# Triangular inverses from single blocks, swapped attention products and aligned tiles in a hybrid decoder block

## The chip, the cores and the metric

The kernel runs on one core of a Trainium2 chip. The metric is the device time of one launch in microseconds (us). A core has TensorE (PE in the profile, its weight loads apart as PEld), VectorE (DVE), ScalarE (ACT), GpSimd (POOL) and SyncE (SP, which here issues the weight DMAs). Each engine works through its own list of instructions in order; semaphores tie the lists together.

## The reference

One layer of a decoder, 256 tokens of width 2048, float32, no batch. Three residual sub-layers, each with an RMSNorm before and after: a token mixer, a cross-attention into 256 memory tokens (4 heads of 128) and a gated MLP of inner width 5632 with a causal convolution of width 3. The mixer projects to three groups of heads of width 64, whose outputs are joined and projected back:

```python
oa = rmsnorm(dilated_attention(q, k, v), attn_out_gain)   # 12 heads, three window patterns, T5 bias
ob = rmsnorm(spatial_gating(zb), sgu_out_gain)            # 8 groups, causal 128x128 matrices
oc = rwkv7_time_mix(zc)                                   # 12 heads
x = concat([oa, ob, oc]) @ w_out

# rwkv7_time_mix, per head, over time:
sa = state @ -kk_t
state = state * w_t + sa * (kk_t * a_t) + v_t * k_t
y_t = state @ r_t
```

Merging the patterns by their softmax denominators is one softmax over all keys, so the kernel takes scores once, adds one bias per head and distance, and gives the first 128 queries 128 keys and the other 128 queries all 256.

## The kernel before, in words

**Main products.** Every weight matrix is read once from memory in blocks of 128x1024 (`raw`, four buffers, issued on SP). ScalarE casts a block to a rounded copy `hi` (L233), VectorE subtracts to get the rest `lo` (L235); three buffers of each. TensorE multiplies hi with both parts of the activation and lo with its high part (lines 265 to 270 with weights loaded and 256 tokens moving, L284 and L286 for the MLP, L306 to L312 with activations loaded and weights moving). A float32 product that is not in this form takes two passes of TensorE; the profile counts passes.

**Lanes.** All other work (norms, attention, gating, the RWKV part) is written as Python generators. After each part of a main unit the class `Lanes` (L120) advances a virtual time; a generator is resumed when that time reaches what its last `yield x` asked for, and each TensorE instruction that it issued adds 0.15. So the program order of every engine is set when the kernel is built: the lanes' work stands between main products, and what follows a `yield` stands some main products later.

**The inverse (L716 to L785).** The RWKV part works in two chunks of 128 tokens for 12 heads, so 24 matrices of 128x128 that are strictly triangular (`BN`) and for which the inverse of one minus the matrix is wanted. `Dg` gathers the 32x32 diagonal blocks of all (L724), and GpSimd clears them in BN (L725). VectorE inverts the diagonal blocks by substitution, all at once (L737 to L742). The result is transposed (Tz, L746), copied block by block into the block-diagonal `ZE` (L749, by copy2, lines 710 to 714, which gives every other copy to ScalarE, L714, and to VectorE, L712). Then come 24 products BN times ZE (L756), whose results ScalarE copies over BN (L758); the untransposed blocks (Te, L752) go into ZE (L763); and three rounds of 24 products each (L774), with 128, 64 and 32 moving columns per matrix, build the inverse, with an addition of ZE on VectorE after each (L778) and a ScalarE copy into BN after the third (L781). Every one of these 96 products loads a full 128x128 matrix.

**Attention (L1016 to L1107).** For three groups of four heads, two heads at a time: scores (L1038), bias and maximum on VectorE (L1043 to L1048), exponentials on ScalarE with their sums (L1049, L1051), three transpositions per head (L1059) and a copy, then three products per head with the transposed probabilities loaded and v moving (64 columns; L1066, L1068, L1070). The result has tokens on partitions; it is divided by the sums (L1074, L1076), squared and summed (L1080). After the third group the total gives the factor of the RMSNorm (L1085, the power on GpSimd, L327), the outputs are scaled by it (L1090), and 12 transpositions (L1097) turn them so that channels lie on partitions, where they are split into high and low part (`oaT`).

**Output projection (mix_out, L1236).** For two column blocks it multiplies the RWKV outputs (`oc`) first, waits for the lanes until the attention output is there, then multiplies that, and so on.

TensorE's order is thus a steady row of main products with the lanes' products in between, and it is the same list on every run.

Of the kernel before, what the change touches and what calls it, by code (L numbers as in the profile page):

```python
# [12 lines left out]
F32 = mybir.dt.float32  # L13
F32R = mybir.dt.float32r
# [158 lines left out]
def hybrid_block(tc, a, out, dbg=None):  # L173
    nc = tc.nc
    dbg = dbg or {}
    with ExitStack() as ctx:
# [7 lines left out]
        uid = [0]  # L184

# [21 lines left out]
        def small(n, tag="small", bufs=16):  # L207
            return mk(cp, tag, bufs, (P, 16))[:, :n]
# [364 lines left out]
        def vt():  # L573
            return mk(mp, "v", 3, (P, 516))

        def oct_():
            return mk(mp, "oc", 6, (P, 516))

        def ocr():
            return view(mk(mp, "oc", 6, (P, 516), F32R)[:, :512], k=2, t=S)  # L580
# [135 lines left out]
        def inverse():  # L716
# [20 lines left out]
            for j in range(1, 31):  # L737
# [5 lines left out]
                if j % 2 == 0:  # L743
                    yield SUBST
            Tz = k4()
# [4 lines left out]
            yield 4.5  # L750
            Te = k4()
            nc.vector.transpose(Te, T)  # L752
            for g in range(6):
                ps = (auxp, auxq)[g % 2]()
                for n in range(4):
                    nc.tensor.matmul(ps[:, n * P:(n + 1) * P], lhsT=BN[:, g * 4 + n, :],  # L756
                                     rhs=ZE[:, g * 4 + n, :], start=True, stop=True)
# [8 lines left out]
            for g0 in (0, 3):  # L766
                G = {g: ZE[:, g * 4:g * 4 + 4, :] for g in range(g0, g0 + 3)}
                for it in range(3):
                    c0 = 32 * (it + 1) if it else 0
                    for g in range(g0, g0 + 3):  # L770
                        ps = (auxp, auxq)[g % 2]()
                        pv = view(ps, h=4, t=P)
                        for n in range(4):
                            nc.tensor.matmul(pv[:, n, c0:], lhsT=BN[:, g * 4 + n, :],  # L774
                                             rhs=G[g][:, n, c0:], start=True, stop=True)
                        if it == 0:
                            G[g] = view(et(), h=4, t=P)
                        nc.vector.tensor_tensor(G[g][:, :, c0:], pv[:, :, c0:],  # L778
                                                ZE[:, g * 4:g * 4 + 4, c0:], op=ALU.add)
                        if it == 2:  # L780
                            nc.scalar.copy(BN[:, g * 4:g * 4 + 4, :], G[g])  # L781
                    yield 0.7
# [233 lines left out]
        def attention():  # L1016
            asq = small(6, "asq", 1)
            oas = []
            b12 = view(mk(rp, "ze", 1, (P, 3072)), h=A_HEADS, x=256)
# [4 lines left out]
            for j in range(3):  # L1024
# [4 lines left out]
                ov = view(po, b=2, h=4, d=64)  # L1029
                den = small(8, "den", 2)  # L1030
                bt = b12[:, 4 * j:4 * j + 4, :]
                for e0 in (0, 2):
# [7 lines left out]
                    nmx = small(4)  # L1040
                    for e in range(2):
# [8 lines left out]
                                             accum_out=den[:, e0 + e:e0 + e + 1])  # L1050
                        nc.scalar.activation(sc[:, 128:384], sc[:, 128:384], AF.Exp,  # L1051
                                             bias=nmx[:, 2 * e + 1:2 * e + 2],
                                             accum_out=den[:, 4 + e0 + e:5 + e0 + e])
                        scs.append(sc)
                    yield 4.5
# [8 lines left out]
                    for e in range(e0, e0 + 2):  # L1064
                        h, pT = 4 * j + e, pts[e - e0]
# [413 lines left out]
```

## Time and profile before

| what | value |
|---|---|
| time, median of 3 runs | 1372.5 us (1372.31 to 1373.0) |
| the profiled execution's own time | 1375.61 us |
| its span | 1373.9 us |
| mean granted TensorE clock | 0.993 |
| VectorE, ScalarE, GpSimd busy | 63%, 52%, 11% of the span |
| DMA | 238.80 MB, mean 174 GB/s |

The span is the time from the first to the last instruction that the profiler saw; the time of the launch is a little longer. PE lines are matrix passes; PEld lines are the loads of the stationary operand ahead of them, which overlap the passes. In rows of a timeline the start and length in us come first, and `x8` stands for eight instructions in one row, so that the distance between the starts of rows gives the pace, while a single recorded length contains the pipeline. In a group's row stand, behind the bar, the busy time in us and the mean length of one in ns. A row of windows has, per engine, busy time and count, then the granted clock as a share of full speed, the DMA share and the GB/s.

### The profile page before, as it was taken

What the parts mean: (1) busy time and instruction counts of PE and PEld (TensorE: products, weight loads), DVE (VectorE), ACT (ScalarE), POOL (GpSimd) and SP (SyncE); (2) the same over time, 40 slices, a digit from 0 to 9 for tenths busy, and PEclk for the clock granted to TensorE, in tenths of its full rate; (3) what the DMA queues carried; (4) which work ended last, traced back from release to release, by engine and by line L of the source; (5) the groups of instructions that cost most, each with busy time, mean ns of one, the idle gap of its engine ahead of it and who ended that gap; (6) DMA issues with size and microseconds to landing.
All of it is one profiled execution on the core that took longest, in us unless ns stands there. A gap on an engine that the chain in (4) does not pass through costs nothing.

```text
span 1373.9 us, 20692 instructions
## 1 busy us (share of the span) xinstructions
PE 1337.0 (97%) x8036; PEld 1175.1 (86%) x8036; DVE 869.4 (63%) x1277; ACT 715.7 (52%) x1097; POOL 149.6 (11%) x185
## 2 busy tenths in 40 slices
PE   6899999999999999999999999999999999999997
PEld 6889989999987879878888888888888888888886
DVE  5579964456555766567767676767676674444444
ACT  5755363244446656456555555555555553434442
POOL 3011100120003110001111111111111120000001
PEclk9999999999999999999999999999999999999999
DMA  7545553145547755444655656666666666556663
GB/s 219 157 137 156 146 173 94 55 148 149 147 142 258 255 181 166 157 148 132 190 185 184 185 186 189 188 188 184 184 186 187 188 218 194 193 195 191 195 196 128
DMA packets 189840, 238.80 MB, mean 174 GB/s; under 512 B 7920, under 2 KB 144013, under 8 KB 189741
## 3 DMA queue, kind: packets, MB, share of 16 engines
q1 hardware_dynamic: 185802, 225.76, 53.1%
q0 software_dynamic: 3376, 11.29, 2.5%
q8 instruction: 63, 1.03, 0.3%
q10 hardware_dynamic: 563, 0.43, 0.1%
q14 instruction: 36, 0.29, 0.1%
HBM read 235.33 MB, written 2.12 MB: 173 GB/s over the span
## 4 chain that ended last, share of the span: by engine, by line
PE 91%; issue 3%; DVE 2%; DMA 1%; ACT 1%; POOL 1%; ACTq 0%; DVEq 0%; POOLq 0%
PE mm L284 24%; PE mm L286 12%; PE mm L306 10%; PE mm L308 10%; PE mm L312 10%; PE mm L265 6%; PE mm L270 5%; PE mm L267 5%; PE auxq L657 1%; DMA wa<-in_rwkv_w_up_dram 1%; DVE lo L235 1%; PE auxq L774 1%; PE auxp L774 1%; DMA raw<-in_w_in_dram 0%; ACT hi L233 0%
## 5 line engine op out<-in xcount | busy, mean ns | idle before, releaser
L235 DVE TENSOR_TENSOR lo<-raw,hi 128x1024 fp32r<-128x1024 f32 x422 | 517.5, 1227 | 392.9 <-ACT hi L233 391.6
L233 ACT CAST hi<-raw 128x1024 fp32r<-128x1024 f32 x422 | 442.9, 1050 | 468.0 <-PE mm L308 171.6
L284 PE MATMUL mm<-h,hi 128*128 128x512 f32 x1376 | 486.3, 399 | 0.0
L286 PE MATMUL mm<-h,lo 128*128 128x256 f32 x1376 | 386.5, 281 | 0.0
L284 PEld LDWEIGHTS mm<-h,hi 128*128 128x128 f32 x1376 | 258.6, 188 | 64.4
L286 PEld LDWEIGHTS mm<-h,lo 128*128 128x128 f32 x1376 | 260.0, 189 | 0.0
L265 PE MATMUL mm<-h,hi 128*128 128x256 f32 x624 | 162.6, 293 | 2.0 <-ACT h L357 2.0
L267 PE MATMUL mm<-h,hi 128*128 128x256 f32 x624 | 160.2, 288 | 0.7 <-DVE h L358 0.7
L308 PE MATMUL mm<-hi,hid 128*128 128x512 f32 x352 | 136.9, 389 | 0.0
L306 PE MATMUL mm<-hi,hid 128*128 128x512 f32 x352 | 136.9, 389 | 0.0
L265 PEld LDWEIGHTS mm<-h,hi 128*128 128x128 f32 x624 | 120.8, 195 | 4.3 <-ACT h L357 2.2
L267 PEld LDWEIGHTS mm<-h,hi 128*128 128x128 f32 x624 | 120.6, 194 | 1.7 <-DVE h L358 1.0
L1419 POOL TENSOR_TENSOR z<-z,rrow 128x256 f32<-128x256 f32 x86 | 70.7, 822 | 427.5 <-DVE z L1418 427.5
L312 PE MATMUL mm<-lo,hid 128*128 128x512 f32 x352 | 108.4, 389 | 0.0
L270 PE MATMUL mm<-h,lo 128*128 128x256 f32 x624 | 102.5, 286 | 0.0
L270 PEld LDWEIGHTS mm<-h,lo 128*128 128x128 f32 x624 | 87.2, 193 | 1.3 <-issue 1.0
L306 PE MATMUL mm<-hi,h 128*128 128x512 f32 (+1 forms) x208 | 79.1, 385 | 1.4 <-ACT hi L233 1.4
L312 PEld LDWEIGHTS mm<-lo,hid 128*128 128x128 f32 x352 | 66.1, 188 | 13.8
L308 PEld LDWEIGHTS mm<-hi,hid 128*128 128x128 f32 x352 | 66.1, 188 | 13.7
L306 PEld LDWEIGHTS mm<-hi,hid 128*128 128x128 f32 x352 | 66.0, 188 | 13.7
L308 PE MATMUL mm<-hi,h 128*128 128x512 f32 (+1 forms) x208 | 77.0, 375 | 0.0
L312 PE MATMUL mm<-lo,h 128*128 128x512 f32 (+1 forms) x208 | 59.8, 375 | 0.2 <-DVE lo L235 0.2
(336 smaller groups left out, 1520.5 us busy)
## 6 DMA issues: line engine op xcount, KB each, us to landing
raw<-in_ffn_w_up_dram SPq DMA_DIRECT2D x176, 512.0 KB, 3.6
raw<-in_w_in_dram SPq DMA_DIRECT2D x94, 512.0 KB, 4.3
raw<-in_ffn_w_down_dram SPq DMA_DIRECT2D x88, 512.0 KB, 4.6
raw<-in_w_out_dram SPq DMA_DIRECT2D x32, 512.0 KB, 5.0
raw<-in_mem_wkv_dram SPq DMA_DIRECT2D x16, 512.0 KB, 4.1
raw<-in_mem_wq_dram SPq DMA_DIRECT2D x8, 512.0 KB, 3.8
raw<-in_mem_wo_dram SPq DMA_DIRECT2D x8, 512.0 KB, 3.7
x<-in_x_dram SPq DMA_DIRECT2D x8, 256.0 KB, 7.4
```

The source lines that it names most:

```text
L233: nc.scalar.copy(hv, rv)
L235: nc.vector.tensor_tensor(lv, rv, hv.bitcast(F32), op=ALU.subtract)
L265: nc.tensor.matmul(o, lhsT=hv[:, k, cs], rhs=X.h(k0 + k), start=(k0 + k == 0), stop=False)
L267: nc.tensor.matmul(o, lhsT=hv[:, k, cs], rhs=X.l(k0 + k), start=False, stop=False)
L270: L.last = nc.tensor.matmul(o, lhsT=lv[:, k, cs], rhs=X.h(k0 + k), start=False, stop=(k0 + k == nk - 1))
L284: nc.tensor.matmul(view(ps[t], z=2, t=S), lhsT=hv[:, k, cs], rhs=X.hl[k0 + k], start=(k0 + k == 0), stop=False)
L286: L.last = nc.tensor.matmul(ps[t][:, S:], lhsT=lv[:, k, cs], rhs=X.h(k0 + k), start=False, stop=(k0 + k == KT - 1))
L306: nc.tensor.matmul(o, lhsT=X.h(kk)[:, ts_], rhs=hv[:, k, :], start=(first and k0 + k == 0), stop=False)
L308: nc.tensor.matmul(o, lhsT=X.l(kk)[:, ts_], rhs=hv[:, k, :], start=False, stop=False)
L312: L.last = nc.tensor.matmul(o, lhsT=X.h(kk)[:, ts_], rhs=lv[:, k, :], start=False, stop=(last and k0 + k == nk - 1))
L774: nc.tensor.matmul(pv[:, n, c0:], lhsT=BN[:, g * 4 + n, :], rhs=G[g][:, n, c0:], start=True, stop=True)
L1419: nc.gpsimd.tensor_tensor(z, z, x2row, op=ALU.mult)
```

## The change

Three things are changed.

1. **Inverse.** BN keeps its off-diagonal blocks, and both the transposed and the plain inverted 32x32 blocks are copied in before the first product (Tz into ZE, Te into BN's diagonal), eight block copies in one place. Then the inverse grows: from pairs of 32x32 blocks to 64x64 by products of single blocks (new lines 766, 777 and 780: 2 and then 3 products of 32x32 per matrix), and from 64x64 to 128x128 (lines 792 and 799: one product of 64x64 each per matrix). Each result is copied out of PSUM by copy2 on 32 or 64 partitions. No adds remain. The `yield`s between the stages are 6.5, 1.5, 1.5, 1.0 and 0.7.
2. **Attention.** The probabilities are multiplied by the reciprocal of their sums before the transposition (due time 5.0 in place of 4.5), the product with v loads v (64 columns) and moves the probabilities (256 and 128 columns), so that the result has channels on partitions and the 12 transpositions at the end go. The sum of squares over channels is now taken by GpSimd additions and a product with a column of ones (new L1111), and its factor is spread over a row by two products (L1119) and multiplied in (VectorE twice, GpSimd once).
3. **Tile layout.** Small tiles are 32 B per partition in place of 64, v and oc tiles 2176 B in place of 2064, and two tiles that nothing uses fill 256 and 480 B, so that the tiles of the mixer and of the right side start at other addresses modulo 64. A program change of one line shifts line numbers: what was L306 is L307, L233 is L234.

```diff
-            return mk(cp, tag, bufs, (P, 16))[:, :n]
+            return mk(cp, tag, bufs, (P, 8))[:, :n]
...
-            return mk(mp, "oc", 6, (P, 516))
+            return mk(mp, "oc", 6, (P, 544))[:, :516]
...
-                nc.gpsimd.memset(BN[q, :, q], 0.0)
...
-            yield 4.5
             Te = k4()
             nc.vector.transpose(Te, T)
-            for g in range(6):
-                ps = (auxp, auxq)[g % 2]()
-                for n in range(4):
-                    nc.tensor.matmul(ps[:, n * P:(n + 1) * P], lhsT=BN[:, g * 4 + n, :],
-                                     rhs=ZE[:, g * 4 + n, :], start=True, stop=True)
-                nc.scalar.copy(BN[:, g * 4:g * 4 + 4, :], view(ps, h=4, t=P))
-                if g % 2:
-                    yield 0.5
             for b in range(4):
                 q = slice(32 * b, 32 * b + 32)
-                copy2(b, ZE[q, :, q], view(Te, n=32, l=32)[q, :, 0:24].rearrange("p n l -> p l n"))
-            yield 3.5
...
+                copy2(b, BN[q, :, q], view(Te, n=32, l=32)[q, :, 0:24].rearrange("p n l -> p l n"))
+            yield 6.5
+
+            E = k4()
+            E = view(E, l=32, m=32)
+            halves = ((0, 16), (16, 24))
+            for h0, h1 in halves:
+                ps = [auxp(), auxq()]
+                for n in range(h0, h1):
+                    for u in range(2):
+                        f, g = slice(64 * u, 64 * u + 32), slice(64 * u + 32, 64 * u + 64)
+                        nc.tensor.matmul(ps[u][g, (n - h0) * 32:(n - h0 + 1) * 32], lhsT=BN[f, n, g], rhs=ZE[f, n, f],
+                                         start=True, stop=True)
+                for u in range(2):
+                    g = slice(64 * u + 32, 64 * u + 64)
+                    copy2(u, E[g, h0:h1, :], ps[u][g, :(h1 - h0) * 32].rearrange("p (l m) -> p l m", m=32))
+            yield 1.5
+            for h0, h1 in halves:
+                ps = [auxp(), auxq()]
+                for n in range(h0, h1):
+                    for u in range(2):
+                        f, g = slice(64 * u, 64 * u + 32), slice(64 * u + 32, 64 * u + 64)
+                        nc.tensor.matmul(ps[u][f, (n - h0) * 32:(n - h0 + 1) * 32], lhsT=E[g, n, :], rhs=BN[g, n, g],
+                                         start=True, stop=True)
+                    f, g = slice(0, 32), slice(32, 64)
+                    nc.tensor.matmul(ps[0][g, (n - h0) * 32:(n - h0 + 1) * 32], lhsT=BN[g, n, g], rhs=E[g, n, :],
+                                     start=True, stop=True)
...
+            lo_, up = slice(0, 64), slice(64, 128)
+            for g in range(3):
+                ps = (auxp, auxq)[g % 2]()
+                for n in range(8 * g, 8 * g + 8):
+                    nc.tensor.matmul(ps[up, (n % 8) * 64:(n % 8 + 1) * 64], lhsT=BN[lo_, n, up], rhs=ZE[lo_, n, lo_],
+                                     start=True, stop=True)
+                copy2(g, ZE[up, 8 * g:8 * g + 8, lo_], ps[up, :].rearrange("p (l m) -> p l m", m=64))
+            yield 1.0
...
+                    rden = small(4)
+                    nc.vector.reciprocal(rden, den)
+                    for e, sc in enumerate(scs):
+                        for b, w in ((0, slice(0, 128)), (1, slice(128, 384))):
+                            nc.vector.tensor_scalar(sc[:, w], sc[:, w], rden[:, 2 * e + b:2 * e + b + 1],
+                                                    None, op0=ALU.mult)
+                    yield 5.0
...
+                    for b, w in ((0, slice(0, S)), (1, slice(P, S))):
+                        for e in range(2):
+                            nc.tensor.matmul(po[64 * e:64 * e + 64, c0 + w.start:c0 + w.stop],
+                                             lhsT=vhead(b, 4 * j + e0 + e),
+                                             rhs=pts[e][:, b * S:b * S + w.stop - w.start],
+                                             start=(b == 0), stop=(b == 1))
...
+                sq = et()
+                nc.scalar.activation(sq, po, AF.Square)
...
+                    for k in range(2):
+                        nc.gpsimd.tensor_tensor(asq, asq, sq[:, k * S:(k + 1) * S], op=ALU.add)
...
+                nc.tensor.matmul(ps[:, b:b + 1], lhsT=asq[:, b * P:(b + 1) * P], rhs=cmask[:, 1, P - 1:P],
+                                 start=True, stop=True)
...
+                nc.tensor.matmul(ps[:, b * P:(b + 1) * P], lhsT=ars[:, b:b + 1].to_broadcast([P, P]), rhs=ident,
+                                 start=True, stop=True)
```

What moves is seen in the engines' lists. On TensorE, in the third part of the inverse, `mm` is the result of a main product, `auxp` and `auxq` those of the lanes. Before:

```order
L308 MATMUL mm_2233<-hi_2324,h_167 128x256
L312 MATMUL mm_2233<-lo_2325,h_155 128x256 x2
L312 MATMUL mm_2233<-lo_2325,h_166 128x256 x2
L774 MATMUL auxp_2352<-ze_1339,BN 128x128 x4
L774 MATMUL auxq_2359<-ze_1339,BN 128x128 x4
L774 MATMUL auxp_2366<-ze_1339,BN 128x128 x4
L306 MATMUL mm_2232<-hi_2375,h_177 128x256
L308 MATMUL mm_2232<-hi_2375,h_178 128x256
```

and now, at the end of the growth to 128:

```order
L309 MATMUL mm_2221<-hi_2424,h_168 128x256
L313 MATMUL mm_2221<-lo_2425,h_156 128x256 x2
L313 MATMUL mm_2221<-lo_2425,h_167 128x256 x2
L792 MATMUL auxp_2440<-ze_1336,BN 64x64 x8
L792 MATMUL auxq_2450<-ze_1336,BN 64x64 x8
L792 MATMUL auxp_2460<-ze_1336,BN 64x64 x8
L307 MATMUL mm_2222<-hi_2424,h_156 128x256
L309 MATMUL mm_2222<-hi_2424,h_157 128x256
```

Before, twelve products of 128x128 stand together, in two such sets of three rounds, after three sets of eight from L756. Now 48 products at L766 stand in one block, then 72 at L777 and L780, 24 at L792 and 24 at L799; between the blocks stand 20, 20 and 10 rows of main products.

On ScalarE, where the block copies stand (k4 tiles are named `k`), before:

```order
L233 CAST hi_2073<-raw_2071 128x1024
L714 COPY ze_1339<-k_340_2173 32x24x32 x2
L587 ACTIVATE zg<-z_2040,omu 128x256
L830 COPY nat_2009<-auxq_2011 128x512
L233 CAST hi_2095<-raw_2093 128x1024
L233 CAST hi_2117<-raw_2115 128x1024
L587 ACTIVATE zg<-z_2044,omu 128x256
```

and now:

```order
L234 CAST hi_2070<-raw_2068 128x1024
L715 COPY ze_1336<-k_340_2170 32x24x32 x2
L588 ACTIVATE zg<-z_2037,omu 128x256
L850 COPY nat_2006<-auxq_2008 128x512
L234 CAST hi_2092<-raw_2090 128x1024
L715 COPY BN<-k_341_2176 32x24x32 x2
L234 CAST hi_2114<-raw_2112 128x1024
L588 ACTIVATE zg<-z_2041,omu 128x256
```

The two copies into BN, which read the transposition Te, come between two casts; their two partners on VectorE come between the two subtractions that belong to these casts.

On TensorE, the product with v of the last pair of heads, before:

```order
L312 MATMUL mm_4066<-lo_4253,h_177 128x512 x2
L1066 MATMUL auxq_4080<-v_2231,et_4236 128x64
L1068 MATMUL auxq_4080<-v_2231,et_4236 128x64
L1070 MATMUL auxq_4080<-v_2231,et_4236 128x64
L1066 MATMUL auxq_4080<-v_2231,et_4242 128x64
L1068 MATMUL auxq_4080<-v_2231,et_4242 128x64
L1070 MATMUL auxq_4080<-v_2231,et_4242 128x64
L306 MATMUL mm_4067<-hi_4252,h_177 128x512
```

and now:

```order
L313 MATMUL mm_4119<-lo_4317,h_178 128x512 x2
L1092 MATMUL auxq_4133<-et_4300,v_2220 64x256
L1092 MATMUL auxq_4133<-et_4306,v_2220 64x256
L1092 MATMUL auxq_4133<-et_4300,v_2220 64x128
L1092 MATMUL auxq_4133<-et_4306,v_2220 64x128
L307 MATMUL mm_4120<-hi_4316,h_178 128x512
```

Six products of two passes became four, with v loaded. Behind them stand 18 main products, and then the sum and the row of the norm:

```order
L1111 MATMUL auxp_4360<-cmask,s_559_3453 128x1 x2
L307 MATMUL mm_4373<-hi_4377,oc_2534 128x512
L309 MATMUL mm_4373<-hi_4377,oc_2535 128x512
L307 MATMUL mm_4373<-hi_4377,oc_2534 128x512
L309 MATMUL mm_4373<-hi_4377,oc_2535 128x512
L313 MATMUL mm_4373<-lo_4378,oc_2534 128x512 x2
L307 MATMUL mm_4374<-hi_4377,oc_2534 128x512
L309 MATMUL mm_4374<-hi_4377,oc_2535 128x512
L307 MATMUL mm_4374<-hi_4377,oc_2534 128x512
L309 MATMUL mm_4374<-hi_4377,oc_2535 128x512
L313 MATMUL mm_4374<-lo_4378,oc_2534 128x512 x2
L1119 MATMUL auxp_4402<-ident,small_4367 128x128 x2
```

Between the two stand 12 main products; the first product that reads the attention output comes 60 products after L1119. From the output projection's memory part on, TensorE's list is as before.

More of the change, by code (lines that the diff above doesn't have):

```diff
@@ L184, in hybrid_block @@
         uid = [0]
+        cp.tile([P, 64], F32, name="fill")
         def nm(s):
@@ L783, in inverse @@
+            for g in range(3):
+                ps = (auxp, auxq)[g % 2]()
+                for n in range(8 * g, 8 * g + 8):
+                    nc.tensor.matmul(ps[lo_, (n % 8) * 64:(n % 8 + 1) * 64], lhsT=ZE[up, n, lo_], rhs=BN[up, n, up],
+                                     start=True, stop=True)
+                copy2(g + 1, BN[lo_, 8 * g:8 * g + 8, up], ps[lo_, :].rearrange("p (l m) -> p l m", m=64))
+            yield 0.7
             for i in range(3):
@@ L1040, in attention @@
                     nmx = small(4)
+                    den = small(4, "den", 2)
                     for e in range(2):
@@ L1072, in attention @@
                 give("col", 2)
-                rden = small(8)
-                nc.vector.reciprocal(rden, den)
                 oa = ca()
-                nc.vector.tensor_tensor(view(oa, q=8, d=64), view(po, q=8, d=64),
-                                        rden.unsqueeze(2).to_broadcast([P, 8, 64]), op=ALU.mult)
-                for b in range(2):
-                    junk = et()
-                    nc.scalar.activation(junk[:, :256], oa[:, b * 256:(b + 1) * 256], AF.Square,
-                                         accum_out=asq[:, b * 3 + j:b * 3 + j + 1])
```

81 lines of the change are left out of this document (32 added, 49 removed).

## The prediction

> **What bounds the kernel now.** The profiled execution took 1375.6 us (span 1373.9); the median of the runs shown is 1372.5, so 3.1 us are taken off at the end. The page first, its busy shares and the head of its chain:
>
> ```profile
> PE 1337.0 (97%) x8036; PEld 1175.1 (86%) x8036; DVE 869.4 (63%) x1277; ACT 715.7 (52%) x1097; POOL 149.6 (11%) x185
> ...
> PE 91%; issue 3%; DVE 2%; DMA 1%; ACT 1%; POOL 1%; ACTq 0%; DVEq 0%; POOLq 0%
> ```
>
> TensorE is busy and on the chain nearly throughout. An average could hide a stage with another limit, so next the windows over the stages that change: block copies, inverse, attention (its length in us, then the busy time of PE, PEld, DVE, ACT and POOL, the clock granted, the DMA share and GB/s):
>
> ```profile
> 150.00:200.00 50.00, 49.20 (x332) 44.41 (x331) 39.06 (x62) 25.88 (x31) 3.38 (x3) 1.00 0.58 169
> 200.00:250.00 50.00, 49.97 (x438) 48.95 (x437) 22.09 (x33) 20.90 (x30) 4.88 (x4) 1.00 0.33 95
> 350.00:400.00 50.00, 50.00 (x371) 45.82 (x371) 31.17 (x61) 23.13 (x48) 0.00 (x0) 1.00 0.51 148
> ```
>
> From 200 to 250 us TensorE has 0.03 us idle and VectorE is busy under half the time. So the products of the inverse cost their TensorE time one for one, and their waits are covered by main products. That is the first question of this change: how much TensorE time does it remove, and the second: which waits does it open.
>
> **The inverse.** Timeline of TensorE (start, length, line): groups of four products, each in two passes (x8).
>
> ```profile
> 195.22 1.06 PE L756 MATMUL auxp<-ze,BN 128*128 128x128 f32 x8
> 196.12 1.06 PE L756 MATMUL auxq<-ze,BN 128*128 128x128 f32 x8
> ...
> 218.20 1.06 PE L774 MATMUL auxq<-et,BN 128*128 128x32 f32 x8
> 219.09 1.06 PE L774 MATMUL auxp<-et,BN 128*128 128x32 f32 x8
> ```
>
> Starts lie 0.90 and 0.89 us apart, 112 ns a pass, though the moving tile has 128 columns in the first and 32 in the second: the 128 loaded columns set the pace. Removed are 24 products at L756 and 72 at L774, 192 passes: 192 x 0.112 = **-21.5 us**. Added are 120 products of 32x32 and 48 of 64x64, so 336 passes. Only one narrow load is in the trace:
>
> ```profile
> L510 PEld LDWEIGHTS auxp<-oneh,tab x2: 84/84/85, 37.6 to 37.6; 32*12 32x12 f32 x2
> ...
> L510 PE MATMUL auxp<-oneh,tab x2: 477/478/478, 37.6 to 37.9; 32*12 32x384 f32 x2
> ...
> 37.60 0.80 PE L510 MATMUL auxp<-oneh,tab 32*12 32x384 f32 x2 [1.89 <-issue]
> ...
> L774 PEld LDWEIGHTS auxp<-et,BN 128*128 128x128 f32 x48 | 5.8, 192 | 0.0
> ```
>
> A load of 12 columns is recorded with 84 ns, one of 128 with 192: (192-84)/116 = 0.93 ns per column, close to 112/128 = 0.875. The second matmul starts 0.80-0.48 = 0.32 us after the first, 0.83 ns per moving column. By columns, then, a 32x32 pass takes 28 ns and a 64x64 pass 56 ns: 240 x 0.028 + 96 x 0.056 = 12.1 us if one follows another. The 32x32 products alternate between two places of the array (rows 0 to 63, 64 to 127). For that the trace has L657, with 64 rows:
>
> ```profile
> 233.33 0.63 PE L270 MATMUL mm<-h,lo 128*128 128x256 f32 x4
> 233.89 0.49 PE L657 MATMUL auxq<-ca,col 64*128 64x128 f32 x4
> 234.21 0.39 PE L657 MATMUL auxq<-col,col 64*128 64x128 f32 x4
> ...
> 234.66 0.39 PE L657 MATMUL auxq<-col,col 64*128 64x128 f32 x4
> 234.98 0.39 PE L265 MATMUL mm<-h,hi 128*128 128x256 f32 x1
> 235.20 0.28 PE L267 MATMUL mm<-h,hi 128*128 128x256 f32 x1
> ```
>
> Eight passes in 234.66-234.21 = 0.45 us are 56 ns a pass, half of 112: two places load side by side. Changing shape costs something: from the start at 233.33 to that at 235.20 are 1.87 us, against 4 x 0.12 (four N=256 starts, (0.63-0.28)/3 apart) + 16 x 0.056 + 0.12 = 1.50, so 0.4 a stage, 1.6 for four. In the first stage each matrix has two such products, in the second three. If those of a matrix run fully side by side, the two stages take 48 x 0.028 each, 2.7 together, and with 5.4 for the 64x64 products and 1.6 they make 9.7; one after another it is 12.1 + 1.6 = 13.7. I take 11.5, near the middle, since only pairs are seen in the trace: **-10.0** (-11.8 to -7.8).
>
> The rule that speaks against this is a fixed price of a pass. The row gives only an upper end: 56 ns a pass or less. The Trainium skill, TensorE: Matmul & The Clock Gate, section "Wait — 56ns, not 53.3ns?", says that starts never come closer than about 25 ns, and with hardware decode off about 62 ns per matmul. By 25 the stages would take 336 x 0.025 + 1.6 = 10.0 us and the whole come to 1362.4, by 62 they would take 22.4 us and the whole come to 1374.8; the trace's 56 ns speaks against the second.
>
> **Eviction copies.** Their nearest row on ScalarE is
>
> ```profile
> L1080 ACT ACTIVATE et<-ca 128x256 f32<-128x256 f32 x6 | 2.5, 413 | 5.7 <-DVE ca L1076 5.7
> ```
>
> so 512 columns take at most 0.83 us. They stand on ScalarE and VectorE in place of the adds and copies of before; by the windows both have half of this stage free, and in the new order 20, 20 and 10 rows of main products lie between the four stages, at 0.12 us or more each. Zero; without that cover each stage would wait for one such copy, 2.5 us in all. The first product ran at 195.22; its inputs will be ready by about 182 (below), so it waits for nothing.
>
> **Block copies at 177 us.** Now the copies of Te also stand here, ahead of a cast (L235 is the subtraction that follows each cast):
>
> ```profile
> L235 DVE TENSOR_TENSOR lo<-raw,hi 128x1024 fp32r<-128x1024 f32 x422 | 517.5, 1227 | 392.9 <-ACT hi L233 391.6
> ...
> 177.26 1.24 DVE L752 STREAM_TRANSPOSE k<-k 128x1024 f32<-128x1024 f32 x1
> ...
> 174.65 1.63 ACT L714 COPY ze<-k 32x768 f32<-32x768 f32 x1
> ...
> 177.19 2.00 ACT L233 CAST hi<-raw 128x1024 fp32r<-128x1024 f32 x2
> ...
> 178.29 0.50 PE L306 MATMUL mm<-hi,h 128*128 128x512 f32 x1 [0.63 <-ACT hi L233]
> 178.63 0.40 PE L308 MATMUL mm<-hi,h 128*128 128x512 f32 x1
> 178.86 0.39 PE L306 MATMUL mm<-hi,h 128*128 128x512 f32 x1
> ...
> 181.61 0.39 PE L306 MATMUL mm<-hi,h 128*128 128x512 f32 x1
> ```
>
> TensorE already waits here for a cast, so nothing is in hand. The second cast, needed at 181.61, ended at 179.19. Now two copies, of 1.63 each as those of Tz, wait for the transposition's end at 178.50, and the cast of 1.00 follows: 178.5 + 3.3 + 1.0 = 182.8, 1.2 us late, and the subtraction on VectorE behind it a little more. **+1.6** (0 if TensorE comes later here than now, 2.5 if the subtraction's 1.2 adds in full).
>
> **Attention, products with v.** Rows of before:
>
> ```profile
> 406.00 0.39 PE L1068 MATMUL auxq<-v,et 128*128 128x64 f32 x2
> ...
> 406.90 0.39 PE L1070 MATMUL auxq<-v,et 128*128 128x64 f32 x2
> ...
> 412.65 0.60 PE L1097 MATMUL auxp<-ident,ca 128*128 128x128 f32 x4
> ```
>
> Eight passes in 0.90 us: 112 each, 72 passes, 8.1 us removed. Added: 12 products with 256 moving columns (0.213 a pass at 0.83 ns) and 12 with 128 (0.106): 24 x 0.213 + 24 x 0.106 = 7.7 us one after another, 3.9 if the two halves of the array (64 columns each) run side by side, plus 6 x 0.4 for the shape: 10.1 or 6.3. The trace shows no such pair in columns: +2.0 to -1.8; L657's pairs in rows are the nearest row, so I take **-1.0**. The 12 transpositions (0.11 each, 1.3) go, two column sums and two row products (0.2 each at most, with a switch) come: **-0.4**.
>
> **Attention, waits.** Each pair of heads now has a reciprocal and four multiplications between its last exponential and its transposition:
>
> ```profile
> 371.94 0.19 ACT L1051 ACTIVATION_READ_ACCUMULATOR et<-et,small 128x1 f32 x1
> ...
> 372.41 0.20 DVE L1074 RECIPROCAL small<-den 128x8 f32<-128x8 f32 x1
> ...
> 374.12 0.82 PE L1059 MATMUL auxp<-ident,et 128*128 128x128 f32 x6
> ...
> L1090 DVE TENSOR_SCALAR ca<-ca,small 128x256 f32<-128x256 f32 x6 | 1.7, 348 | 0.8 <-POOL small L327 0.8
> ```
>
> The exponentials of this pair ended at 372.13 and TensorE came at 374.12, 2.0 in hand; the step needs 0.2 + 0.35 + at most 0.35 for the first head, about 1.0 with the hand-over. The last three of the six pairs have such room; the first three have hardly any, but get one more main unit in front (due time 5.0 for 4.5). **+0.8** (0 to 6 x 1.3, were a subtraction of 1.2 us in front each time).
>
> **Norm chain.** After the last product a Square of 512 columns, two POOL additions, the column sum, the power and the row are in series. Prices, beside that of L1080:
>
> ```profile
> 411.16 0.70 POOL L327 TENSOR_TENSOR small<-small,mhalf 128x2 f32<-128x2 f32 x1 [77.60 <-DVE small L322]
> ...
> L1419 POOL TENSOR_TENSOR z<-z,rrow 128x256 f32<-128x256 f32 x86 | 70.7, 822 | 427.5 <-DVE z L1418 427.5
> ```
>
> Square at most 0.83, additions 2 x 0.82, hand-overs: 3 us against 18 main products of 0.23, 4.1. The power 0.70 with two small VectorE steps: 2 to 3.6 us against 12 main products, 2.7. The last multiplications have 60 products (13.6 us) in front of their reader. **+0.4** (0 to 2).
>
> **Tile starts and clock.** Tiles move by 32 B; the main products on oc, 80 of each of three kinds, pace as the others do:
>
> ```profile
> L306 PE MATMUL mm<-hi,oc 128*128 128x512 f32 x80 | 31.8, 402 | 0.0
> ...
> 259.00:262.30 3.30, 2.72 (x24) 2.50 (x24) 2.65 (x8) 1.21 (x13) 1.01 (x1) 1.00 0.15 19
> 262.30:265.70 3.40, 3.40 (x20) 3.18 (x21) 2.32 (x8) 0.34 (x4) 1.17 (x1) 0.50 0.37 136
> ```
>
> A start worth 5 ns would make 240 x 0.005 = 1.2: 0 (+-1.2). The clock was 0.50 for 3.4 us behind a stretch with TensorE 82% busy; a window more or less is 1.7: 0 (+-1.7).
>
> **Sum.** -10.0 + 1.6 - 1.0 - 0.4 + 0.8 + 0.4 = -8.6; 1375.6 - 8.6 = 1367.0, less 3.1: **1363.9**. Best ends: -11.8 - 1.8 - 0.4 - 1.2 - 1.7 = -16.9, so 1355.6.
>
> **Rivals.**
> - *A pass has a price of its own.* At L657's 56 ns: 336 x 0.056 + 1.6 = 20.4, the inverse gains 1.1 and the time is 1372.8. That 56 is half of a load's 112, so it looks like the load and not like a floor: 0.07.
> - *Slower: a narrow load costs a full one.* 336 x 0.112 + 1.6 = 39.2 us in the inverse, 17.7 more than before: 1391.6. Every pass price over (21.5 - 1.6 + 1.3)/0.336 = 63 ns makes the kernel slower by over 0.2%. Against it: the record of 84 ns for 12 columns. 0.05.
> - *The gain is given back by waits*: attention 7.8, norm 2.0, copies 2.5 make 12.3 against 11.4 gained: 1373.4. The places with no room (three pairs of heads, the cast at 178) speak for it, the added main units against. 0.12.
> - *The clock falls in the inverse.* Small products leave the array idle between, as before 262.3; six windows of 1.7 are 10.2: 1374.1. TensorE has main products between all stages. 0.08.
>
> **How the numbers follow.** The forecast has 0.68. The range goes from the best end to 1375.2, the bound of slower, and so takes in the rivals of waits and clock; what lies beyond is the slow rival and the tails. A measurement tells 0.2% (2.7 us) from no change: faster is below 1369.8. From the forecast 0.63, from the wait rival 0.05, others 0.03: 0.71; same 0.17; slower 0.12.
>
> **What would show it.** The stages at the new L766 to L799 should take 9.7 to 13.7 us of TensorE with starts 28 (32x32) and 56 ns (64x64) apart or pairs; at 178 to 183 a longer TensorE wait for a cast; at the transpositions of attention no wait over 1 us. Starts at 60 ns or more in the inverse, a clock row of 0.50 there, or waits of over 6 us in attention would make the forecast wrong.

## The result, and the profile after

The changed kernel took 1366.27 us (median of 5 runs, 1361.83 to 1366.51), the kernel before 1372.31 (5 runs, 1369.76 to 1373.0): a ratio of 0.9939, 95% interval 0.9922 to 0.9956 (the two medians alone give 0.9956, the end of that interval). On the chip of the first experiments it was 1363.01 against 1373.56, 0.9926 (0.991 to 0.9941). The two profiled executions lie at 1366.33 and 1375.61 us.

The page of the changed kernel first, busy shares and the head of the chain:

```profile
PE 1325.8 (97%) x8152; PEld 1158.8 (85%) x8152; DVE 872.5 (64%) x1292; ACT 710.8 (52%) x1083; POOL 153.8 (11%) x187
...
PE 88%; issue 4%; DVE 3%; DMA 1%; POOL 1%; ACT 1%; ACTq 0%; DVEq 0%; POOLq 0%
```

TensorE is busy 11.2 us less, with 116 passes more. The windows of the three stages (length, busy time of PE, PEld, DVE, ACT, POOL, clock, DMA):

```profile
150.00:200.00 50.00, 48.10 (x315) 42.58 (x315) 41.81 (x68) 27.47 (x30) 3.37 (x3) 1.00 0.56 161
200.00:250.00 50.00, 49.37 (x679) 46.92 (x677) 22.30 (x42) 16.61 (x48) 7.97 (x7) 1.00 0.31 91
350.00:400.00 50.00, 50.00 (x335) 42.53 (x334) 35.73 (x75) 22.62 (x47) 1.78 (x3) 1.00 0.50 150
```

In the first window TensorE now idles 1.9 us instead of 0.8: the block copies. In the second it runs 679 passes where it ran 438.

The inverse on TensorE's timeline: the ends of the main products in front, the first and the last passes of the first stage, the main products on both sides of the second, and the third stage by its line.

```profile
199.92 0.64 PE L313 MATMUL mm<-lo,h 128*128 128x256 f32 x4
200.49 0.21 PE L766 MATMUL auxp<-ze,BN 32*32 32x32 f32 x1
200.49 0.21 PE L766 MATMUL auxq<-ze,BN 32*32 32x32 f32 x1
...
202.00 0.19 PE L766 MATMUL auxq<-ze,BN 32*32 32x32 f32 x1
202.12 0.38 PE L307 MATMUL mm<-hi,h 128*128 128x256 f32 x1
...
204.61 0.64 PE L313 MATMUL mm<-lo,h 128*128 128x256 f32 x4
...
207.18 0.39 PE L307 MATMUL mm<-hi,h 128*128 128x256 f32 x1
...
L792 PE MATMUL auxp<-ze,BN x32: 218/218/267, 210.3 to 213.0; 64*64 64x64 f32 x32
```

96 passes start between 200.49 and 202.00: 16 ns apart, in pairs. The whole stage, from the last main product's start (200.28) to the next (202.12) less its own 0.12, is 1.72 us; the second, 144 passes between main products that start at 204.97 and 207.18, is 2.09. In the third, 48 passes start in 2.8 us, 58 ns apart. Summed in this way, the products of the inverse took 20.7 us before and take 1.72 + 2.09 + 3.03 + 3.03 = 9.9 now.

To see where the rest went, the same main passes are looked up in both traces (6832 in each) and their starts compared; the table has what each stretch of before gained (-) or lost in us. The first column counts from the first of these passes, which itself starts 0.3 to 0.9 us earlier in these kernels than in before. The parts alone are the experiments below.

| kernel | to 60 us | 60-170 | 170-192 | 192-300 | 300-400 | 400-470 | behind |
|---|---|---|---|---|---|---|---|
| changed | +2.9 | 0.0 | +1.7 | -10.0 | -2.4 | -1.1 | +0.4 |
| layout alone | -2.5 | +0.1 | 0.0 | +0.1 | +0.2 | -0.8 | +0.3 |
| inverse alone | +0.1 | -0.1 | +1.8 | -10.1 | -1.5 | -0.7 | -0.4 |
| attention alone | -1.6 | 0.0 | 0.0 | -1.6 | -1.2 | -1.1 | -0.4 |
| changed, once more | +0.2 | 0.0 | +1.7 | -10.3 | -2.4 | -0.8 | +0.4 |

Three things in the table are not the change, or not surely. The first is the clock: windows over the start of the changed kernel, and then of before (length, PE busy, clock, DMA).

```profile
18.70:22.10 3.40, 3.24 (x16) 0.50 0.85 232
39.10:42.50 3.40, 3.40 (x19) 0.59 0.49 158
```

```profile
18.70:22.10 3.40, 2.61 (x14) 0.68 0.82 239
39.10:42.50 3.40, 3.40 (x31) 1.00 0.45 149
262.30:265.70 3.40, 3.40 (x20) 0.50 0.37 136
```

The code up to 60 us does the same work in both; the half-clock stretches fall elsewhere from run to run (in the changed kernel's second profile at 53 to 57 us). The second, less surely: before's stretch at 262 us, 1.7 us, has no counterpart in the profile of the changed kernel, and of -10.0 some 1.7 are that. Of the three profiles with the old inverse, two have such a stretch (the layout alone at 259 us) and the attention alone has none; of the nine with the new inverse, none has. So the change may have a part in it, which these runs don't settle. The third is a wait for a cast in before's profile,

```profile
436.53 0.50 PE L306 MATMUL mm<-hi,h 128*128 128x512 f32 x1 [0.76 <-ACT hi L233]
```

which no later profile has in this size: with the layout alone, where TensorE's list is the same, the same pass waits 0.14 us, in the changed kernel not at all, and in one run below 0.40. The five runs of the changed kernel spread over 4.7 us, of which the clock at the start is the likely reason. What the change itself does is the table from 60 to 470 us, -11.8, less these 1.7 and 0.8: about -9.3 us.

One border of the table needs care. With the new inverse the other products of the lanes stand in other groups: a group of scores (1.0 us) that stood behind before's pass at 300 us now stands ahead of it, so that about 1 us of gain shows in the next column, in the row of the inverse alone too. The products' 10.8 and the clock's 1.7 would make 12.5 in the column of the inverse; with four transpositions of the gating that crossed the border too, 1.3 of the missing 2.5 are found, and the rest lies in the new grouping, which no run separates.

### The profile page after: what moved, and what is told of

Read it like the earlier page. It is cut to its first block, busy times and chain, and to the rows that moved or that the text cites. A ratio compares the mean times of both kernels' runs of the same rounds, so it can differ in the third digit from the quotient of the medians.

```text
span 1364.6 us, 20906 instructions
## 1 busy us (share of the span) xinstructions
PE 1325.8 (97%) x8152; PEld 1158.8 (85%) x8152; DVE 872.5 (64%) x1292; ACT 710.8 (52%) x1083; POOL 153.8 (11%) x187
## 4 chain that ended last, share of the span: by engine, by line
PE 88%; issue 4%; DVE 3%; DMA 1%; POOL 1%; ACT 1%; ACTq 0%; DVEq 0%; POOLq 0%
PE mm L285 24%; PE mm L287 12%; PE mm L307 10%; PE mm L309 10%; PE mm L313 10%; PE mm L271 5%; PE mm L266 5%; PE mm L268 5%; DVE lo L236 1%; DMA wa<-in_rwkv_w_up_dram 1%; PE auxq L658 1%; DMA raw<-in_w_in_dram 0%; PE auxp L1056 0%; DVE row L1327 0%; PE auxq L916 0%
## 5 line engine op out<-in xcount | busy, mean ns | idle before, releaser
L234 ACT CAST hi<-raw 128x1024 fp32r<-128x1024 f32 x422 | 443.1, 1051 | 463.6 <-PE mm L285 170.8
L307 PE MATMUL mm<-hi,hid 128*128 128x512 f32 x352 | 136.9, 389 | 0.0
L307 PE MATMUL mm<-hi,h 128*128 128x512 f32 (+1 forms) x208 | 79.2, 386 | 1.7 <-ACT hi L234 1.7
L309 PEld LDWEIGHTS mm<-hi,hid 128*128 128x128 f32 x352 | 66.1, 188 | 13.8
L307 PEld LDWEIGHTS mm<-hi,hid 128*128 128x128 f32 x352 | 66.1, 188 | 13.7
```

Source lines behind the costliest of these rows:

```text
L234: nc.scalar.copy(hv, rv)
L307: nc.tensor.matmul(o, lhsT=X.h(kk)[:, ts_], rhs=hv[:, k, :], start=(first and k0 + k == 0), stop=False)
L309: nc.tensor.matmul(o, lhsT=X.l(kk)[:, ts_], rhs=hv[:, k, :], start=False, stop=False)
```

## The experiments

**The three parts alone, and the whole again.** Each is the kernel before with one numbered part of the change; the tile layout is

```diff
+        cp.tile([P, 64], F32, name="fill")
...
-            return mk(cp, tag, bufs, (P, 16))[:, :n]
+            return mk(cp, tag, bufs, (P, 8))[:, :n]
...
-            return mk(mp, "v", 3, (P, 516))
+            return mk(mp, "v", 3, (P, 544))[:, :516]
```

and the same for oc and `fill2`.

> The kernel before with the tile layout of the change alone. Theory (the gain is TensorE passes that are gone): tile starts cost nothing, so the time stays within 1.2 us of before, TensorE's list is the same and main products on oc still start 0.23 us apart. Rival (the starts carry the gain): 3 us or more faster, with shorter passes or shorter VectorE operations in the mixer.

1372.36 against 1373.56 us, 0.9992 (0.9981 to 1.0002), and in the table nothing differs but the start and the wait at 436 us: the starts are worth nothing that shows.

The inverse alone:

> The kernel before with the new inverse alone. Theory: TensorE's time in the products of the inverse falls from 20.7 to 9.9 us as in the changed kernel, and the wait for a cast behind the block copies costs 1.8; between the main products at 170 and 300 us the kernel gains 9.0 us, and the whole is 7 to 10 us faster, up to 3 more or less by the clock of the first 45 us. Rival (the products were partly hidden, or the new attention brings half of the gain): 5 us faster or less.

1364.31 us, 0.9934 (0.9919 to 0.9949), 9 us faster. The stages take 9.7 us and the wait at the block copies is there (+1.8). The inverse alone carries most of what the whole gains, 9.3 of 10.6 us.

The attention alone:

> The kernel before with the new attention alone. Theory: scores and products with v save 1.7 us of TensorE time, sums and row in place of the 12 transpositions 0.2, and the wait in front of the gating's transpositions costs 1.0 to 1.2: 0.3 to 1.5 us faster, too little for the whole time to show. Rival (waits of the new normalization give back more than that): 2 us or more slower, with TensorE waits in front of the transpositions of the probabilities.

1370.85 us, 0.9985 (0.9973 to 0.9997): 2.7 faster, more than I expected, with an interval from 0.4 to 3.7. By the table it gains 2.3 from 300 to 470 us, 0.8 of it before's wait at 436, so 1.5, the upper end of what I named. TensorE's waits between 165 and 460 us in it begin with the one named:

```profile
PE auxq L1178 <- DVE et L1169: 1.0, 1, 1.0
```

> The changed kernel once more, beside the three parts on the same chip. Theory: 6 to 10 us faster than before; the three parts add up to it within 2 us where the clock of the first 45 us is alike. Rival (the parts work on each other): the sum of the parts is off by 3 us or more.

-1.2, -9.3 and -2.7 add up to -13.2; the whole gives -10.6. The difference of 2.6 is within the 3 us that were allowed and the spread of the runs, but not within the 2 that I named; the table from 60 to 470 us does add up: -15.0 for the parts, and with before's clock stretch taken once instead of twice and its wait at 436 us once instead of three times -11.7, against -11.8 for the whole.

**Do places of the array load side by side?** The 32x32 products in another order:

```diff
-                for n in range(h0, h1):
-                    for u in range(2):
+                for u in range(2):
+                    for n in range(h0, h1):
```

in both stages, and the third product of a matrix in a loop of its own.

> The changed kernel with the 32x32 products of the inverse in another order: within a half, first all of one place of the array, then all of the next, instead of the places in turn. Theory (places load side by side; one place takes 28 ns a pass): the first stage grows from 1.7 to 96 x 0.028 + 0.4 = 3.1 us, the second from 2.1 to 144 x 0.028 + 0.4 = 4.4, together 3.7 us slower than the changed kernel. Rival (the pace of 15 to 16 ns a pass is that of a single place or of the issue, and the places don't matter): no change.

1368.99 us, 0.9962 (0.9948 to 0.9977), some 5 us slower than the changed kernel's 1363 to 1364. The first stage takes 2.9 us instead of 1.7, the second 4.3 instead of 2.1: 3.4 more, where the theory had 3.7. The starts within one place lie 32 ns apart. Where one place ends and the other begins, its timeline shows something more:

```profile
197.38 0.44 PE L766 MATMUL auxp<-ze,BN 32*32 32x32 f32 x9
197.64 0.21 PE L766 MATMUL auxq<-ze,BN 32*32 32x32 f32 x1
197.67 0.19 PE L766 MATMUL auxp<-ze,BN 32*32 32x32 f32 x1
197.69 0.19 PE L766 MATMUL auxq<-ze,BN 32*32 32x32 f32 x1
```

All `auxp` products stand before the first `auxq` one in TensorE's list, and yet three `auxq` passes start among the last of `auxp`: the free place began while the other still worked off what was ahead.

**The products with v, one half of the columns at a time.**

```diff
-                    for b, w in ((0, slice(0, S)), (1, slice(P, S))):
-                        for e in range(2):
+                    for e in range(2):
+                        for b, w in ((0, slice(0, S)), (1, slice(P, S))):
```

> The changed kernel with the products with v ordered head by head, so that neighbours use the same half of the array's columns. Theory (the two column halves run side by side, 7 ns apart): each of the six groups grows by one half's worth, 2 x 0.213 + 2 x 0.106 = 0.64 us, together 3.8 us slower than the changed kernel. Rival (moving columns share one path, so that the halves only start together): no change.

1363.96 us, 0.9929 (0.9913 to 0.9946): no slower, so my expectation fell. Between 300 and 400 us it even gains 2.9 us on before where the changed kernel gains 2.4; the half microsecond comes at one group, in which the second head's inputs are late (the last experiment shows it). But the halves do run side by side. One group in this kernel, and one in the changed kernel:

```profile
395.19 0.88 PE L1092 MATMUL auxq<-et,v 128*64 128x256 f32 x8
396.00 0.50 PE L307 MATMUL mm<-hi,h 128*128 128x512 f32 x1
```

```profile
397.31 0.87 PE L1092 MATMUL auxq<-et,v 128*64 128x256 f32 x8
```

The eight passes need 0.81 us from start to next start; one after another the moving columns alone are 4 x 0.213 + 4 x 0.106 = 1.28. With the overlap seen in the run before, four passes of one half do not hold up the other half's: the order within so short a group doesn't matter; that is argued, not shown. The edit did not separate the halves, and so it could not test what I meant it to.

**The wait behind the block copies.** In the changed kernel:

```profile
180.50 3.25 ACT L715 COPY BN<-k 32x768 f32<-32x768 f32 x2 [0.29 <-DVE k L752]
...
183.77 1.04 ACT L234 CAST hi<-raw 128x1024 fp32r<-128x1024 f32 x1
...
184.87 0.50 PE L307 MATMUL mm<-hi,h 128*128 128x512 f32 x1 [1.14 <-ACT hi L234]
```

Two copies, the cast behind them, and TensorE 1.14 us late, as the prediction's chain had it. First the copies were given to GpSimd:

```diff
-                copy2(b, BN[q, :, q], view(Te, n=32, l=32)[q, :, 0:24].rearrange("p n l -> p l n"))
+                nc.gpsimd.tensor_copy(BN[q, :, q], view(Te, n=32, l=32)[q, :, 0:24].rearrange("p n l -> p l n"))
```

> The changed kernel with the four block copies of Te on GpSimd instead of ScalarE and VectorE. Theory (the copies ahead of the cast are what TensorE waits for at 185 us): that wait of 1.1 us goes, and the second block's cast is back in time; four copies of some 2.5 us on GpSimd end before the first product at 200 us: 1.1 to 1.8 us faster than the changed kernel in the main products from 180 to 190 us. Rival (GpSimd's copies slow VectorE, or another wait comes there): less than 0.5 us faster, with longer subtractions on VectorE between 180 and 190 us.

1364.86 us, 0.9939 (0.9922 to 0.9955): no gain, and between 170 and 192 us it loses 2.9 us to before, 1.2 more than the changed kernel. The rival holds. Its timeline:

```profile
178.19 1.18 DVE L236 TENSOR_TENSOR lo<-raw,hi 128x1024 fp32r<-128x1024 f32 x1
178.33 8.38 POOL L755 COPY BN<-k 32x768 f32<-32x768 f32 x4
179.62 2.30 DVE L236 TENSOR_TENSOR lo<-raw,hi 128x1024 fp32r<-128x1024 f32 x1
181.84 1.82 DVE L589 SCALAR_TENSOR_TENSOR zg<-z,par,zg 128x255 f32<-128x255 f32 x1
...
183.70 0.63 ACT L1011 ACTIVATE zg<-zg 128x512 f32<-128x512 f32 x1 [2.15 <-DVE zg L589]
184.23 2.92 ACT L234 CAST hi<-raw 128x1024 fp32r<-128x1024 f32 x3
185.29 4.77 DVE L236 TENSOR_TENSOR lo<-raw,hi 128x1024 fp32r<-128x1024 f32 x3 [1.63 <-ACT hi L234]
...
185.31 0.50 PE L307 MATMUL mm<-hi,h 128*128 128x512 f32 x1 [1.08 <-ACT hi L234]
...
187.84 0.73 PE L313 MATMUL mm<-lo,h 128*128 128x512 f32 x2 [1.33 <-DVE lo L236]
```

While GpSimd copies, the subtraction takes 2.30 us instead of 1.18 and a step of 0.48 takes 1.82. The wait for the cast, which was to go, stays at 1.08 us: the cast now stands behind a ScalarE step (183.70) that waited 2.15 us for that slowed VectorE step. And the first subtraction from 185.29 on, beside the last copy, takes 2.50 us and costs TensorE another 1.33. The Trainium skill, SBUF — State Buffer, section "SBUF: two separate sides", says that VectorE and GpSimd contend for one pair of ports that a whole instruction holds; these rows agree with it: the first of the four copies, taken by itself, runs from 178.33 to 180.82, and the subtraction that started beside it at 179.62 ends 1.10 us after that.

**The wait at the gating's transpositions.** The changed kernel around 413 us:

```profile
411.62 1.66 DVE L359 SCALAR_TENSOR_TENSOR h<-ca,par,h 128x256 fp32r<-128x256 f32 x4
413.21 0.14 DVE L323 TENSOR_SCALAR small<-small 128x1 f32<-128x1 f32 x1
413.43 0.54 POOL L328 TENSOR_TENSOR small<-small,mhalf 128x1 f32<-128x1 f32 x1 [4.35 <-DVE small L323]
414.00 0.49 DVE L1189 TENSOR_SCALAR et<-et,small 128x512 f32<-128x512 f32 x1 [0.66 <-POOL small L328]
...
414.55 0.44 PE L1198 MATMUL auxq<-ident,et 128*128 128x128 f32 x2 [0.99 <-DVE et L1189]
```

Four steps of the attention output's splitting (L359) stand in front of a step of 0.14 us on which the gating's power, its multiplication and two transpositions hang. The edit puts that chain ahead:

```diff
-                nc.scalar.activation(junk, mx_, AF.Square, accum_out=bsq)
-                rs = rstd_of(bsq, 1, 1.0 / B_W, 1e-6)
-                nc.vector.tensor_scalar(mx_, mx_, rs, None, op0=ALU.mult)
+                with tc.high_priority(offset=AHEAD):
+                    nc.scalar.activation(junk, mx_, AF.Square, accum_out=bsq)
+                    rs = rstd_of(bsq, 1, 1.0 / B_W, 1e-6)
+                    nc.vector.tensor_scalar(mx_, mx_, rs, None, op0=ALU.mult)
```

> The changed kernel with the last normalization of the gating group ahead of the attention's splitting in the lists of ScalarE, VectorE and GpSimd. Theory (the splitting of the attention output, now in one burst, stands ahead of the small operations that TensorE's gating transpositions wait for): the wait of 1.0 us goes and nothing takes its place, 1.0 us faster than the changed kernel between 400 and 430 us. Rival (the chain itself is late, from its square to the multiplication): the wait stays at 0.5 us or more.

1361.97 us, 0.9916 (0.9901 to 0.9931). The wait is gone: the two places of L1198 cost 0.7 us of TensorE time instead of 1.9, as L1170 did before the change. But in this profile most of the 1.2 us is given back 14 us later:

```profile
422.93 0.50 PE L307 MATMUL mm<-hi,h 128*128 128x512 f32 x1 [0.40 <-ACT hi L234]
```

This is the pass at which before's profile waited (436.53 there), and from 435 to 440 us of before this run gains 1.0 and 0.8 us less than the changed kernel in its two profiles. The next run has the same edit and no wait at this pass, so the edit need not bring it.

**Both waits gone.** The same, and the copies of Te held back:

```diff
+            yield 2.0
             for b in range(4):
                 q = slice(32 * b, 32 * b + 32)
-                copy2(b, BN[q, :, q], view(Te, n=32, l=32)[q, :, 0:24].rearrange("p n l -> p l n"))
-            yield 6.5
+                with tc.issue_after((L.rest if b % 2 else L.cast).ins):
+                    copy2(b, BN[q, :, q], view(Te, n=32, l=32)[q, :, 0:24].rearrange("p n l -> p l n"))
+            yield 4.5
```

where `L.cast` and `L.rest` are the last cast and subtraction of `split`.

> The changed kernel with the gating normalization ahead as in the run before, and the four block copies of Te held back behind three more casts and subtractions, still on ScalarE and VectorE. Theory (only their place ahead of the cast costs): the wait of 1.1 us at 185 us and the one for the subtraction behind it go, TensorE's main products gain 1.2 to 1.8 us between 178 and 190 us over the changed kernel and 1.2 us between 400 and 430 us, and nothing comes in their place: 2.4 to 3.0 us faster than the changed kernel where the clock is alike. Rival (the copies wait or hold up others wherever they stand): as the run with the gating ahead alone, 1.2 us faster than the changed kernel.

1360.47 us, 0.9900 (0.9887 to 0.9912): faster than before by 13.8 us, and than the changed kernel by some 3 (0.9926 there). ScalarE now copies between later casts, and of TensorE's waits for casts only before's own 0.6 is left (first row of this kernel's waits, then of the changed kernel's):

```profile
186.33 3.29 ACT L715 COPY BN<-k 32x768 f32<-32x768 f32 x2
```

```profile
PE mm L307 <- ACT hi L234: 0.6, 1, 0.6
```

```profile
PE mm L307 <- ACT hi L234: 1.7, 2, 1.1
PE auxq L1198 <- DVE et L1189: 1.0, 1, 1.0
```

From 170 to 192 us it is level with before (-0.1 where the changed kernel has +1.7). So the copies cost by their place alone. Between 400 and 470 us this run gains 2.0 us on before, where the changed kernel gains 1.1 and 0.8 in its two profiles: here the gating's 1.2 us come through. Not all of the 3 us are the two waits, though: from 192 to 300 us the run gains 10.9 us where the changed kernel gains 10.0 and 10.3, with the lanes' products in other groups there.

**The normalization of the probabilities.**

```diff
-                    for e, sc in enumerate(scs):
-                        for b, w in ((0, slice(0, 128)), (1, slice(128, 384))):
-                            nc.vector.tensor_scalar(sc[:, w], sc[:, w], rden[:, 2 * e + b:2 * e + b + 1],
-                                                    None, op0=ALU.mult)
```

> The changed kernel without the four multiplications that normalize the probabilities of each pair of heads; the softmax is left without its division. TensorE's transpositions then stand earlier in its list. Theory (the normalization is hidden behind main products): TensorE's time in and around the transpositions of the probabilities stays at 3.5 to 3.7 us, and the whole is within 0.8 us of the changed kernel between 300 and 410 us. Rival (the new multiplications give back part of the gain by waits): 2 us or more faster there.

1363.26 us, 0.9914 (0.9901 to 0.9928), too near to the changed kernel for the whole to tell. Between 300 and 400 us it gains 3.5 on before where the changed kernel gains 2.4: 1.1 us, between the two expectations and nearer to the first. Most of it is one place. In the changed kernel:

```profile
356.55 1.21 DVE L236 TENSOR_TENSOR lo<-raw,hi 128x1024 fp32r<-128x1024 f32 x1
357.69 0.55 DVE L1086 COPY et<-auxp 128x384 f32<-128x384 f32 x1
...
357.85 0.65 PE L1092 MATMUL auxq<-et,v 128*64 128x256 f32 x2
...
358.43 0.49 PE L1056 MATMUL auxp<-col,col 64*128 64x128 f32 x2
...
358.84 0.86 PE L1092 MATMUL auxq<-et,v 128*64 128x256 f32 x6
```

The second head's transposed probabilities are copied at 357.69, behind a subtraction of 1.21; the other products with v start at 358.84. This group takes 2.7 us of TensorE time, the two like it 1.75; without the normalization all three take 1.75.

## Why the prediction was right, and which terms were off

The forecast was 1363.9; measured were 1366.3 and, on another chip, 1363.0. Term by term, by TensorE time and by the stretches of the table:

- **Products of the inverse, -10.0: measured -10.8**, and the inverse alone carries most of the gain. The pace by loaded columns held (32 ns for 32 columns where I had 28, 58 for 64 where I had 56), and so did the side-by-side end of the range: with places in turn a stage takes 1.7 us, in one place 2.9. I had put the value between the ends for want of a row; the stages came to 9.9, the best end was 9.7. The rival of a price of 56 ns or more a pass is refuted by 96 passes in 1.5 us, and so is that of a full load's price, by 58 ns for 64 columns where 128 take 112. No half-clock stretch came in the inverse: the clock was 1.00 from 150 to 250 us. By the lower figure of the Trainium skill (TensorE: Matmul & The Clock Gate, section "Wait — 56ns, not 53.3ns?"), 25 ns, the stages would by estimate have taken 10.0 us, which is near, but the starts come closer here, 16 ns on average over two places; within one place they keep to 32.
- **Block copies, +1.6: measured +1.7 to +1.8**, by the chain that was predicted, and gone when the copies stand elsewhere.
- **Products with v, -1.0: measured about -2.6**, the mis-sized term, beyond its best end of -1.8. A pair of heads took 1.26 us (three groups that stand by themselves, 3.8 together) and takes 0.89; where scores follow directly, 2.2 and 1.75. Both halves run together, and the 0.4 for changing shape that I added to each group isn't to be seen: 0.81 from start to next start is 2 x 0.213 + 2 x 0.106 and less than 0.2.
- **Transpositions against sums and row, -0.4: measured -0.2** (1.1 before; 0.5 and 0.4 now).
- **Attention's waits, +0.8: measured about 1.1**, at one of the pairs, with a subtraction in front as the upper end had it. It stands in front of the products with v, though; in front of the transpositions, where it was forecast, no wait shows. The reason that I gave for the first three pairs, the due time of 5.0, can't be the whole: without the normalization, at the same due time, the transpositions of two pairs stand 3 to 12 main passes earlier in TensorE's list. What the due time alone does, no run shows.
- **Norm chain, +0.4: measured 0.1 at the sum's own place, but 1.2 at the gating's transpositions**. The size lies within the bounds (0 to 2), but the place wasn't named: I had looked at who waits for the norm, not at whom the splitting behind it holds up on VectorE.
- **Tile starts, 0**: 0.9992 by the layout alone.
- **Clock**: the profiled runs differ by +2.9 at the start and -1.7 at 262 us. Of the 2.4 us between forecast and first median this is the likely reason, since the changed kernel's two profiles differ by as much there (+2.9 and +0.2) and hardly anywhere else; which run gets how many half-clock stretches stays open.

The rival of waits that give the gain back had the places nearly right (cast, heads, norm) and the sum wrong: 1.7 + 1.1 + 1.2 = 4.0 us, not 12.3, against 13.6 gained.

So the mechanism was right, and the nearness of the sum is in part luck: the products of the inverse and with v gave 2.4 us more than forecast, copies, waits, norm and transpositions took 1.5 us more.

## What to carry to other kernels

Where TensorE is saturated, count what a product loads: a small block costs its own columns (32 ns for 32), and blocks in different places of the array, taken in turn, cost half of that or less: 16 ns a pass with two places, 13 with three. When work is gathered into one place of a list, look at what stands behind it on that engine: here two gathered bursts of a few us, neither of them on TensorE's path, made TensorE wait 1.1 and 1.0 us by the cast and the 0.14-us step behind them, and both waits went by a change of order alone. Look also at whether the engine to which such a burst is moved shares something with the one that was to be freed.

## What the runs showed of the hardware

- Passes in different places of the array overtake each other. In the run with one place at a time, passes of the second place started while up to three passes that stand ahead of them had not (197.64 against 197.67). The Trainium skill, TensorE: Matmul & The Clock Gate, section "The mechanism", says that matmuls start and end strictly in program order; by these starts they don't across places.
- Two passes whose weights fill different halves of the columns run side by side with 256 moving columns each: 0.81 us for eight passes that would take 1.28 in turn.
- GpSimd copies between SBUF tiles slow VectorE's two-input steps to between twice and four times their time (1.18 to 2.30, 0.48 to 1.82 us).
- Between executions of one kernel the half-clock stretches of the first 60 us move, and with them 2 to 3 us of the total.
